# A two-layer attention trunk on one core: the high and low halves of the stationary weights stored column by column in turn

## The chip, the core and the metric

The kernel runs on one core of a Trainium2 chip. The metric is the device time of one execution in microseconds, lower is better. Before the change it is 277.55 us, the median of three runs (277.17 to 279.52). A profiled execution of the same program gives one trace, and the rows further down are read from it.

## The reference

The input is 256 tokens of 1024 features. Two mixer layers follow each other, each ending in a residual layer normalization. In short:

```python
def mla_mixer(x, ...):                  # layer A
    h = x @ w_in                        # 1024 -> 768 + 256 + 32 + 1024
    c_q, c_kv, k_rope, gate = split(h)
    q = rms_norm(c_q) @ w_uq            # 16 heads of 64 + 32
    kv = rms_norm(c_kv) @ w_ukv         # 16 heads of 64 (key) + 64 (value)
    o = causal_softmax_attention(q, k, v)
    return (o * silu(gate)) @ w_o
def moba_mixer(x, ...):                 # layer B, keys and values from x after layer A
    q, gate = split(x @ w_in)           # 1024 -> 1024 + 1024
    o = causal_softmax_attention(rope(q), rope(x @ w_k), x @ w_v)
    return (o * silu(gate)) @ w_o
x = layer_norm(2 ** 0.5 * x + mixer(x)) # ALPHA = 4 ** 0.25
```

With 256 tokens and blocks of 256 the block selection of layer B selects nothing beyond a token's own block, so the kernel computes a causal attention there.

## The kernel before

**Three passes for a product.** TensorE multiplies in a reduced float32 (`fp32r`). To keep accuracy each operand is split into a high half h, rounded to that type, and a low half l, the rest; a product is the sum of three matmuls, h·h, h·l and l·h. The helper `split` (line 445 and the lines around it) makes the halves: ScalarE copies the source into h with the rounding (line 397), then VectorE or GpSimd subtracts h from the source into l (line 408). `passes` (around line 434) issues the three matmuls, all of them recorded under line 427.

**Two kinds of products.** In a `chunk` the weights are the stationary operand: 128 columns of the weights are loaded into the array, and 256 token columns of the activations stream past. Its three loads are h, h and l of the weights. The matmul groups `g1`, `ga`, `qr`, `kq`, `qb`, `kb` and `gb` are of this kind; a matmul of theirs has 256 streamed columns. In `token_products` (`uv`, `oa`, `vb`, `ob`) the activations are stationary, and the weights stream past, 512 columns in most matmuls. For `oa` and `ob` the stationary operand is the gated attention output, kept as `big_h` and `big_l`; for `uv` and `vb` it is `act_h` and `act_l`, which the change leaves alone.

**Weights.** `weights` walks through a list of units (`ORDER`) of 128 partitions by 1024 columns (768 for `qr`, 512 for `kr`). A DMA on SP's queue loads a unit into one of five `raw` buffers, `split` writes h into one of six buffers named `wh` and l into one of six named `wl`. Within a buffer the columns lie side by side, 4 bytes apart, and begin at an offset that depends on the kind of unit (`AT_W`, 8 to 24 elements). The unit `kr` is an exception: its h and l lie in runs of 64 columns in one `wh` buffer. The last two units of `oa`, `vb` and `ob` go into `x_h` and `x_l`.

**Order.** All operations are recorded first, with a table of which view each writes and reads. `Schedule.order` then lists them by a cost model, and each engine's queue runs in the listed order. GpSimd has eight of the sixteen subtractions into `big_l` (the entries `og` of the table `POOL`) and none of the weights'.

Of the kernel before, what the change touches and what calls it, by code (L numbers as in the profile page):

```python
# [8 lines left out]
F32R = mybir.dt.float32r  # L9
# [4 lines left out]
P = 128  # L14
D = 1024
S = 256
# [6 lines left out]
SCALE_B = 64.0 ** -0.5  # L23
# [5 lines left out]
HL_BUFS = 6  # L29
G_BUFS = 5  # L30
LAG = 8
# [20 lines left out]
HEAT = 12  # L52
PAIR = 1.1

AT_ACT, AT_W = 8, {"g1": 24, "ga": 24, "qr": 10, "kq": 10, "qb": 10, "kb": 10, "gb": 10, "uv": 8, "oa": 8, "vb": 8, "ob": 8}
SHIFT = ("x_h", "x_l", "act_h", "act_l", "big_h", "big_l", "wh", "wl")
PLAIN = 2
PIECES = 4
LATE = 2000
# [4 lines left out]
def on(*key):  # L64
    return "pool" if key in POOL else "dve"
# [3 lines left out]
class Val:  # L69
# [9 lines left out]
    def tile(self):  # L79
        if self.t is None:  # L80
            if self.bank:
                self.t = self.pool.tile(self.shape, self.dtype, tag=self.tag, name=self.tag, bufs=self.bufs)
            else:

                n, line = int(np.prod(self.shape[1:])), 64 if self.dtype is BF16 else 32
                room = -(-n // line) * line + line * (self.tag in SHIFT)
                t = self.pool.tile([P, room], self.dtype, tag=self.tag, name=self.tag, bufs=self.bufs)[:, self.at0:self.at0 + n]
                if len(self.shape) > 2:
                    names = "abc"[:len(self.shape) - 1]
                    t = t.rearrange("p (%s) -> p %s" % (" ".join(names), " ".join(names)), **dict(zip(names[1:], self.shape[2:])))  # L90
                self.t = t
        return self.t
# [272 lines left out]
def trunk(ctx, tc, W0, xtok, W, gq, gkv, lng, lnb, cosa, sina, coska, sinka, cosb, sinb, maskd, identd, out):  # L365
# [3 lines left out]
    wp = ctx.enter_context(tc.tile_pool(name="wp", bufs=1))  # L369
# [85 lines left out]
    U = {name: u for u, name in enumerate(ORDER)}  # L455
    hls = {}
    extra = {}
    state = {"raw": 0, "hl": 0}
    raws = {}

    def load_raw():
# [13 lines left out]
    def weights(name, k):  # L475
        u = U[name, k]
        while state["hl"] <= u:
            v = state["hl"]
            if v not in raws:
                load_raw()  # L480
            nm, kk = ORDER[v]
            n = {"qr": 768, "kr": 512}.get(nm, 1024)
            if nm == "kr":
                hl = sc.val(wp, [P, 1024], F32R, "wh", HL_BUFS).rearrange("p (a b c) -> p a b c", b=2, c=64)
                r = raws.pop(v)[:, 0:n].rearrange("p (a c) -> p a c", c=64)
                split(hl[:, :, 0, :].at(0), hl[:, :, 1, :].at(1), r, n)
                hls[v] = hl.rearrange("p a b c -> p a (b c)")
                state["hl"] += 1
                continue
            if nm in ("oa", "vb", "ob") and kk >= 6:  # L490
                if kk == 6:
                    extra["h"] = C([P, 2, 1024], "x_h", F32R, AT_W[nm])
                    extra["l"] = C([P, 2, 1024], "x_l", F32R, AT_W[nm])
                h, l = extra["h"][:, kk - 6].at(kk), extra["l"][:, kk - 6].at(kk)
            else:
                h = sc.val(wp, [P, 1024], F32R, "wh", HL_BUFS, AT_W[nm])[:, :]
                l = sc.val(wp, [P, 1024], F32R, "wl", HL_BUFS, AT_W[nm])[:, :]
            r = raws.pop(v)
            parts = [(c, c + S) for c in range(S * (v < PLAIN), n, S)] if v < PIECES else [(0, n)]
            for c0, c1 in parts:  # L500
                cs, rs = slice(c0, c1), slice(c0 + S * (v < 8), c1 + S * (v < 8))
                split(h[:, cs].at((kk, c0)), l[:, cs].at((kk, c0)), r[:, rs].at(512 if v < PLAIN else 0), c1 - c0, eng=on("w", nm, kk))
            hls[v] = (h, l, kk, v < PIECES)
            state["hl"] += 1
        return hls[u]

    def wsl(w, c0, c1):
        h, l, kk, early = w
        key = (kk, c0 // S * S if early else 0)
        return h[:, c0:c1].at(key), l[:, c0:c1].at(key)  # L510


    def const(src, shape, name, rows=None):
# [55 lines left out]
    g1 = [bank("s"), bank("s"), bank("pt"), bank("pt")]  # L569
# [8 lines left out]
    for k in range(8):  # L578
        w = weights("g1", k)
        a, b = xs(k)  # L580
        for c in range(8):
# [5 lines left out]
            h, l = wsl(w, c * P, (c + 1) * P)  # L587
# [37 lines left out]
    for j in range(6):  # L625
        b, c = 1 + j // 2, j % 2
# [139 lines left out]
            r.append(t)  # L766
        return r

    def values(la, ps_, pts, Vt, ogh, ogl):

        ps, calls, used = bank("pv"), [], []
        for j, p in enumerate(ps_):
            for t in range(2):
                for s in range(2):
                    v = Vt[:, t, 2 * p + s, :].at((t, (2 * p + s) // 8))
                    calls.append((ps[64 * s:64 * s + 64, j * S + t * P:j * S + S], v, pts[j][s][:, t * S:S + t * P], t == 0, t == 1))
                    used += [v, pts[j][s]]
        mms(calls, ps, used, 250 + 642 * len(ps_))
        for j, p in enumerate(ps_):
            oa = T([P, S], "oa")  # L780
            tt(oa, ps[:, j * S:(j + 1) * S], Gs.pop(p), ALU.mult, S)
            split(ogh[:, p, :].at(p), ogl[:, p, :].at(p), oa, S, eng=on("og", la, p))

    def value_evac(Vt, banks, tok):
        for hf in range(2):
            src = banks[hf].rearrange("p (a b) -> p a b", b=64)
            act(Vt[:, tok, 8 * hf:8 * hf + 8, :].at((tok, hf)), src, 512)

    def attention(la, heads, fill, scale, Vt, ogh, ogl):
        done = []  # L790
        for i in range(8):
            hd, keys = heads(i)
            es = scores(la, i, hd, keys, scale)
            fill(i)
            if len(done) == 2:
                values(la, (i - 2, i - 1), done, Vt, ogh, ogl)
                done = []
            done.append(transp(es))
        values(la, (6, 7), done, Vt, ogh, ogl)

    def heads_mla(p):
        b = p % 4
# [3 lines left out]
    sca = row_power(qsq, 768, "sca")  # L806
    ts(sca, sca, -SCALE_A, None, ALU.mult, None, 2, "pool")
    masks = const(maskd, [P, S], "masks")
    ogh, ogl = C([P, 8, S], "big_h", F32R, AT_ACT), C([P, 8, S], "big_l", F32R, AT_ACT)
    kq_mla(0)  # L810
    kq_mla(1)
    V = C([P, 2, H, 64], "V")
# [10 lines left out]
            else:  # L823
                gate("ga", i, xs)

    attention("a", heads_mla, fill_a, [sca[:, 1:2], sca[:, 0:1]], V, ogh, ogl)


    def load_ln(layer):
# [16 lines left out]
        for hf, cs in enumerate(cols):  # L846
            stt(z[:, cs].at(hf), z[:, cs].at(hf), mv[:, 3:4].at(2), bb[:, cs], ALU.mult, ALU.add, 512)

    def lhs_of(th, tl):
        return lambda k, tok: tuple(t[:, k, tok * P:(tok + 1) * P].at(k) for t in (th, tl))  # L850

    x1h, x1l = C([P, 8, S], "act_h", F32R, AT_ACT), C([P, 8, S], "act_l", F32R, AT_ACT)
    gb, bb = load_ln(0)
# [18 lines left out]
    def x1s(k):  # L872
        return x1h[:, k, :], x1l[:, k, :]

    token_products("oa", 8, lhs_of(ogh, ogl), (("proj", "proj"), ("s", "s")), LAG, finish_a)
    VB = C([P, 2, H, 64], "V")
    token_products("vb", 8, lhs_x1, (("proj", "proj"), ("pv", "proj")), LAG, lambda tok, bk: value_evac(VB, bk, tok))
    gb, bb = load_ln(1)
# [45 lines left out]
    ogh2, ogl2 = C([P, 8, S], "big_h", F32R, AT_ACT), C([P, 8, S], "big_l", F32R, AT_ACT)  # L924

    def fill_b(step):
        for nm, i in PLAN_B[step + 1]:
# [5 lines left out]
        move_heads(step)  # L933

    fill_b(-1)
    attention("b", heads_moba, fill_b, [-SCALE_B, -SCALE_B], VB, ogh2, ogl2)

    def finish_b(tok, bk):
        layer_norm(bk, x1[tok], x1[tok], gb, bb)
# [38 lines left out]
    token_products("ob", 8, lhs_of(ogh2, ogl2), (("proj", "proj"), ("s", "s", "proj")), LAG, finish_b, last_b)  # L978
    sc.emit()


# [89 lines left out]
```

## Time and profile before

| what | value |
|---|---|
| median of 3 runs | 277.55 us (277.17 to 279.52) |
| the profiled execution | 277.43 us |
| its span in the trace | 275.3 us |
| around the span | 2.1 us |
| TensorE, matmuls (PE) | 265.9 us busy, 97% of the span, 1948 matmuls |
| TensorE, weight loads (PEld) | 244.8 us busy, 89%, 1948 loads |
| VectorE (DVE) | 209.2 us, 76% |
| ScalarE (ACT) | 159.8 us, 58% |
| GpSimd (POOL) | 56.7 us, 21% |

A matmul's record is longer than the time by which it holds up the next one, because matmuls overlap in the array. So the pace of TensorE is read from the number of matmuls in a stretch of time, not from the length of one. Each matmul has a weight load of its own, whose record lies beside the matmul ahead of it.

### The profile page before, as it was taken

How to read it: one execution, taken by the hardware profiler on the slowest of the kernel's cores; microseconds unless marked ns; L12 is line 12 of the kernel's file. 1: busy time of each engine (PE TensorE's matmuls, PEld its weight loads, DVE VectorE, ACT ScalarE, POOL GpSimd, SP SyncE). 2: the span in 40 equal slices, each digit the busy share in tenths (PEclk: the TensorE clock that was granted, in tenths of full speed). 3: DMA queues.
4: the chain of work that ended last, by engine and by line, in shares of the span. 5: the costliest groups of instructions: out<-in, count | busy, mean ns of one | idle time of the engine just before them, and what ended most of it. 6: DMA issues, size and time to landing. Idle time of an engine off the chain costs nothing.

```text
span 275.3 us, 5378 instructions
## 1 busy us (share of the span) xinstructions
PE 265.9 (97%) x1948; PEld 244.8 (89%) x1948; DVE 209.2 (76%) x458; ACT 159.8 (58%) x338; POOL 56.7 (21%) x72
## 2 busy tenths in 40 slices
PE   8999999999999999999999999999999999999990
PEld 6999999899899998788878899999999999887880
DVE  2778798999986668828995727869888978684655
ACT  4767877686766678706244734547746858592000
POOL 3000163300130253001010000604133446321100
PEclk9999999999999999999999999999999999999996
DMA  7999855786426342232689776467769577430012
GB/s 235 388 393 341 300 166 177 226 270 192 155 77 195 120 148 76 97 134 79 207 267 339 219 267 185 161 170 226 240 160 353 143 276 243 118 103 2 0 76 76
DMA packets 18681, 52.31 MB, mean 190 GB/s; under 512 B 2912, under 2 KB 6112, under 8 KB 18656
## 3 DMA queue, kind: packets, MB, share of 16 engines
q1 hardware_dynamic: 18656, 51.98, 56.8%
q8 instruction: 15, 0.25, 0.4%
q14 instruction: 10, 0.08, 0.1%
HBM read 45.68 MB, written 1.05 MB: 170 GB/s over the span
## 4 chain that ended last, share of the span: by engine, by line
PE 89%; DVE 5%; DMA 1%; ACT 1%; issue 1%; SPq 0%; POOL 0%; DVEq 0%
PE proj L427 58%; PE s L427 15%; PE pv L427 8%; PE pt L427 4%; PE pt L441 4%; DVE wl L408 2%; DMA kq<-x_h 1%; DVE m L412 1%; DVE act_h L412 1%; SPq L389 0%; DVE bst L840 0%; ACT wh L397 0%; POOL mv L408 0%; ACT pt L397 0%; DVE act_l L408 0%
## 5 line engine op out<-in xcount | busy, mean ns | idle before, releaser
L408 DVE TENSOR_TENSOR wl<-raw,wh 128x1024 fp32r<-128x1024 f32 (+2 forms) x82 | 87.6, 1086 | 22.3 <-ACT wh L397 22.0
L397 ACT CAST wh<-raw 128x1024 fp32r<-128x1024 f32 (+3 forms) x83 | 75.5, 923 | 36.9 <-PE proj L427 15.7
L427 PE MATMUL proj<-act_h,wh 128*128 128x256 f32 x280 | 79.9, 285 | 0.0
L427 PE MATMUL proj<-act_h,wl 128*128 128x256 f32 x280 | 78.4, 280 | 0.0
L427 PE MATMUL proj<-act_l,wh 128*128 128x256 f32 x280 | 78.2, 279 | 0.0
L427 PEld LDWEIGHTS proj<-act_l,wh 128*128 128x128 f32 x280 | 52.9, 189 | 0.0
L427 PEld LDWEIGHTS proj<-act_h,wl 128*128 128x128 f32 x280 | 52.6, 188 | 0.0
L427 PEld LDWEIGHTS proj<-act_h,wh 128*128 128x128 f32 x280 | 52.6, 188 | 0.0
L401 ACT ACTIVATE e<-e,st 128x256 f32<-128x256 f32 x64 | 28.6, 450 | 8.8 <-DVE st L746 8.4
L421 POOL TENSOR_SCALAR e<-e,st 128x256 f32<-128x256 f32 (+1 forms) x32 | 16.0, 515 | 49.1 <-PE s L427 24.6
L427 PE MATMUL s<-kq 128*128 128x256 f32 (+1 forms) x100 | 18.9, 316 | 0.5 <-DMA kq<-x_h 0.5
L427 PE MATMUL proj<-x_h,wh 128*128 128x256 f32 x64 | 18.7, 292 | 0.0
L427 PE MATMUL proj<-x_l,wh 128*128 128x256 f32 x64 | 18.0, 281 | 0.0
L427 PE MATMUL proj<-x_h,wl 128*128 128x256 f32 x64 | 17.9, 280 | 0.0
L427 PEld LDWEIGHTS s<-kq 128*128 128x128 f32 x100 | 15.7, 190 | 2.0 <-PE pt L441 0.7
L397 ACT COPY pt<-pt 128x384 f32<-128x384 f32 x32 | 14.8, 474 | 3.5 <-PE pt L441 3.5
L441 PE MATMUL pt<-ident,e 128*128 128x128 f32 x96 | 15.1, 275 | 0.0
L408 POOL TENSOR_TENSOR t<-t,t512b 128x512 f32<-128x512 f32 x5 | 6.8, 1365 | 31.6 <-DVE t L408 13.9
L746 DVE CUSTOM_DVE_ANT_0 e<-s,masks,sca 128x256 f32<-128x256 f32 (+1 forms) x32 | 11.9, 412 | 1.7 <-POOL e L421 0.5
L408 DVE TENSOR_TENSOR x_l<-raw,x_h 128x256 fp32r<-128x256 f32 (+1 forms) x14 | 10.4, 764 | 3.5 <-ACT x_h L397 3.4
L408 POOL TENSOR_TENSOR mv<-mv,mhalf 128x1 f32<-128x1 f32 x4 | 3.5, 870 | 44.3 <-DVE mv L419 36.1
L408 POOL TENSOR_TENSOR x_h<-t,x_h 128x512 fp32r<-128x512 f32 x7 | 11.0, 1589 | 7.3 <-ACT x_h L397 4.0
(166 smaller groups left out, 567.1 us busy)
## 6 DMA issues: line engine op xcount, KB each, us to landing
raw<-in_W SPq DMA_DIRECT2D x66, 512.0 KB, 4.6
raw<-in_W SPq DMA_DIRECT2D x6, 640.0 KB, 7.4
raw<-in_W SPq DMA_DIRECT2D x6, 384.0 KB, 4.0
kq<-x_h SPq DMA_DIRECT2D x24, 96.0 KB, 2.2
kq<-x_h SPq DMA_DIRECT2D x24, 64.0 KB, 2.1
lng<-in_lng SPq DMA_DIRECT2D x2, 512.0 KB, 3.6
lnb<-in_lnb SPq DMA_DIRECT2D x2, 512.0 KB, 5.0
raw<-in_xtok SPq DMA_DIRECT2D x2, 512.0 KB, 3.7
```

Of the source, the lines that this page charges most:

```text
L397: nc.scalar.copy(A(o), A(i))
L401: nc.scalar.activation(A(o), A(i), func, bias=A(bias), scale=A(scale), accum_out=A(accum))
L408: sc.op(eng, dur, lambda: e.tensor_tensor(A(o), A(a), A(b), op=op), [a, b], [o], lock=not (is_ps(a) or is_ps(b)))
L412: sc.op("dve", dur, lambda: nc.vector.scalar_tensor_tensor(A(o), A(a), A(s), A(b), op0=op0, op1=op1), [a, s, b], [o], lock=not (is_ps(a) o ...
L421: fn = lambda: e.tensor_scalar(A(o), A(a), A(s1), s2, op0=op0, op1=op1)
L427: nc.tensor.matmul(A(out_), A(lt), A(rh), start=st, stop=sp_, skip_group_check=True)
L441: nc.tensor.transpose(A(x), A(y), A(ident))
L746: nc.vector.tensor_tensor_reduce(A(e[:, cs]), A(ps[:, cs]), A(msk), scale=A(scale[b]), scalar=3.0e38, op0=ALU.add, op1=ALU.min, accum_out= ...
```

## The change

The two rings `wh` and `wl` become one ring `w` of six buffers with 2048 columns each. In units whose weights are stationary, h and l of a column are neighbours: h of column c lies at element 2c, l at 2c + 1, so that the columns of either half are 8 bytes apart. The unit's start within its buffer is no longer set by its kind but by the number of the buffer: 0, 12, 22, 32, 44 or 54 elements, that is 0, 48, 88, 128, 176 or 216 bytes. Units whose weights stream past (`uv`, `oa`, `vb`, `ob`) keep two contiguous halves in their buffer. The gated attention output becomes one tensor `big` with h and l in turn in the same way; it is the stationary operand of `oa` and `ob`.

Every engine has the same instructions in the same order as before, with other names and addresses. One thing about the waits differs: in eight of VectorE's subtractions into l, and in one of ScalarE's instructions, a wait for TensorE is no longer listed, since h and l now lie in one buffer and an earlier instruction already waits for it.

```diff
-AT_ACT, AT_W = 8, {"g1": 24, "ga": 24, "qr": 10, "kq": 10, "qb": 10, "kb": 10, "gb": 10, "uv": 8, "oa": 8, "vb": 8, "ob": 8}
-SHIFT = ("x_h", "x_l", "act_h", "act_l", "big_h", "big_l", "wh", "wl")
+AT_ACT, AT_W = 8, 8
+PHASE = (0, 12, 22, 32, 44, 54)
+SHIFT = ("x_h", "x_l", "act_h", "act_l", "big")
...
-                room = -(-n // line) * line + line * (self.tag in SHIFT)
+                room = -(-n // line) * line + line * (self.tag in SHIFT) + 64 * (self.tag == "w")
...
-                hl = sc.val(wp, [P, 1024], F32R, "wh", HL_BUFS).rearrange("p (a b c) -> p a b c", b=2, c=64)
+                hl = sc.val(wp, [P, 2048], F32R, "w", HL_BUFS)[:, 0:1024].rearrange("p (a b c) -> p a b c", b=2, c=64)
+                state["used"] += 1
...
-                h = sc.val(wp, [P, 1024], F32R, "wh", HL_BUFS, AT_W[nm])[:, :]
-                l = sc.val(wp, [P, 1024], F32R, "wl", HL_BUFS, AT_W[nm])[:, :]
+                token = nm in ("uv", "oa", "vb", "ob")
+                t = sc.val(wp, [P, 2048], F32R, "w", HL_BUFS, AT_W if token else PHASE[state["used"] % HL_BUFS])
+                state["used"] += 1
+                t = t.rearrange("p (b c) -> p b c" if token else "p (c b) -> p b c", b=2)
+                h, l = t[:, 0], t[:, 1]
...
-            split(ogh[:, p, :].at(p), ogl[:, p, :].at(p), oa, S, eng=on("og", la, p))
+            split(og[:, p, :, 0].at((p, 0)), og[:, p, :, 1].at((p, 1)), oa, S, eng=on("og", la, p))
...
-    ogh, ogl = C([P, 8, S], "big_h", F32R, AT_ACT), C([P, 8, S], "big_l", F32R, AT_ACT)
+    og = C([P, 8, S, 2], "big", F32R, AT_ACT)
...
-    def lhs_of(th, tl):
-        return lambda k, tok: tuple(t[:, k, tok * P:(tok + 1) * P].at(k) for t in (th, tl))
+    def lhs_of(t):
+        return lambda k, tok: tuple(t[:, k, tok * P:(tok + 1) * P, i].at((k, i)) for i in range(2))
```

## Rows read from the trace of the kernel before

**Rows 1.** The page: busy time of each engine; granted clock by slices; the chain.

```profile
PE 265.9 (97%) x1948; PEld 244.8 (89%) x1948; DVE 209.2 (76%) x458; ACT 159.8 (58%) x338; POOL 56.7 (21%) x72
...
PEclk9999999999999999999999999999999999999996
...
PE 89%; DVE 5%; DMA 1%; ACT 1%; issue 1%; SPq 0%; POOL 0%; DVEq 0%
```

**Rows 2.** Pieces of the chain in order of time: start, length in us, what.

```profile
71.26 1.31 PE s L427 x8
...
123.64 5.59 PE s L427 x24
...
144.96 4.86 PE proj L427 x21
...
159.55 26.52 PE proj L427 x225
...
265.00 2.83 PE proj L427 x24
```

**Rows 3.** Timeline at 44 us, TensorE: start, length in us, engine, instructions merged.

```profile
44.05 0.53 PEld L427 LDWEIGHTS proj<-ones,lnb 128*128 128x128 f32 x4
44.16 0.50 PE L427 MATMUL proj<-ones,lnb 128*128 128x1 f32 x4
```

**Rows 4.** Groups by form, weight loads: count, busy us, mean ns of one.

```profile
L427 PEld LDWEIGHTS proj<-act_h,wh 128*128 128x128 f32 x280 | 52.6, 188 | 0.0
...
L427 PEld LDWEIGHTS pv<-pt,V 128*64 128x64 f32 x128 | 7.9, 136 | 3.8 <-issue 0.7
```

**Rows 5.** Groups by form, matmuls with stationary weights; each stands for three.

```profile
L427 PE MATMUL proj<-act_h,wh 128*128 128x256 f32 x280 | 79.9, 285 | 0.0
...
L427 PE MATMUL proj<-x_h,wh 128*128 128x256 f32 x64 | 18.7, 292 | 0.0
...
L427 PE MATMUL pt<-x_h,wh 128*128 128x256 f32 x32 | 8.8, 280 | 0.0
...
L427 PE MATMUL s<-x_h,wh 128*128 128x256 f32 x28 | 8.0, 290 | 0.0
```

**Rows 6.** Groups by form on VectorE, ScalarE and GpSimd: splits and their like.

```profile
L408 DVE TENSOR_TENSOR wl<-raw,wh 128x1024 fp32r<-128x1024 f32 x64 | 78.8, 1240 | 20.1 <-ACT wh L397 19.9
...
L408 DVE TENSOR_TENSOR wl<-raw,wh 128x256 fp32r<-128x256 f32 x14 | 5.0, 419 | 2.1 <-ACT wh L397 2.1
...
L397 ACT CAST wh<-raw 128x1024 fp32r<-128x1024 f32 x64 | 67.0, 1047 | 34.5 <-PE proj L427 15.7 <-PE s L427 9.1 <-DMA raw<-in_W 6.6
...
L408 POOL TENSOR_TENSOR t<-t,t512b 128x512 f32<-128x512 f32 x5 | 6.8, 1365 | 31.6 <-DVE t L408 13.9 <-DVE st L752 9.2 <-DVE t512b L408 8.4
...
L408 POOL TENSOR_TENSOR big_l<-oa,big_h 128x256 fp32r<-128x256 f32 x8 | 6.5, 824 | 18.8 <-ACT big_h L397 18.8
```

**Rows 7.** Busy time by stages; columns PE, PEld, DVE, ACT, POOL, clock, DMA.

```profile
0.00:28.00 28.00, 26.96 (x207) 25.58 (x208) 18.51 (x38) 18.65 (x37) 2.08 (x6) 1.00 0.92 338
28.00:56.00 28.00, 28.00 (x216) 26.97 (x216) 24.82 (x39) 20.45 (x34) 9.28 (x7) 1.00 0.64 211
56.00:110.00 54.00, 54.00 (x442) 51.28 (x442) 44.58 (x129) 39.60 (x107) 10.89 (x22) 1.00 0.49 156
...
158.00:243.00 85.00, 84.53 (x720) 82.25 (x719) 66.11 (x161) 52.26 (x118) 30.16 (x32) 1.00 0.66 210
```

**Rows 8.** The same stages, VectorE's subtractions into `wl` alone.

```profile
28.00:56.00 28.00, 10.49 (x10) 1.00 0.64 211
56.00:110.00 54.00, 16.77 (x14) 1.00 0.49 156
...
158.00:243.00 85.00, 30.30 (x24) 1.00 0.66 210
```

**Rows 9.** Who waited for whom: us in total, times, longest.

```profile
DVE wl L408 <- ACT wh L397: 22.0, 26, 4.2
...
ACT wh L397 <- PE proj L427: 15.7, 12, 2.1
```

More of the change, by code (lines that the diff above doesn't have):

```diff
@@ L457, in trunk @@
     extra = {}
-    state = {"raw": 0, "hl": 0}
+    state = {"raw": 0, "hl": 0, "used": 0}
     raws = {}
@@ L491, in weights @@
                 if kk == 6:
-                    extra["h"] = C([P, 2, 1024], "x_h", F32R, AT_W[nm])
-                    extra["l"] = C([P, 2, 1024], "x_l", F32R, AT_W[nm])
+                    extra["h"] = C([P, 2, 1024], "x_h", F32R, AT_W)
+                    extra["l"] = C([P, 2, 1024], "x_l", F32R, AT_W)
                 h, l = extra["h"][:, kk - 6].at(kk), extra["l"][:, kk - 6].at(kk)
             else:
-                h = sc.val(wp, [P, 1024], F32R, "wh", HL_BUFS, AT_W[nm])[:, :]
-                l = sc.val(wp, [P, 1024], F32R, "wl", HL_BUFS, AT_W[nm])[:, :]
+                token = nm in ("uv", "oa", "vb", "ob")
[3 more added lines that the diff above has]
+                h, l = t[:, 0], t[:, 1]
             r = raws.pop(v)
@@ L501, in weights @@
                 cs, rs = slice(c0, c1), slice(c0 + S * (v < 8), c1 + S * (v < 8))
-                split(h[:, cs].at((kk, c0)), l[:, cs].at((kk, c0)), r[:, rs].at(512 if v < PLAIN else 0), c1 - c0, eng=on("w", nm, kk))
+                split(h[:, cs].at((kk, c0, 0)), l[:, cs].at((kk, c0, 1)), r[:, rs].at(512 if v < PLAIN else 0), c1 - c0, eng=on("w", nm, kk))
             hls[v] = (h, l, kk, v < PIECES)
@@ L509, in wsl @@
         key = (kk, c0 // S * S if early else 0)
-        return h[:, c0:c1].at(key), l[:, c0:c1].at(key)
+        return h[:, c0:c1].at(key + (0,)), l[:, c0:c1].at(key + (1,))
     def const(src, shape, name, rows=None):
@@ L767, in transp, with values @@
         return r
-    def values(la, ps_, pts, Vt, ogh, ogl):
+    def values(la, ps_, pts, Vt, og):
         ps, calls, used = bank("pv"), [], []
@@ L787, in value_evac, with attention @@
             act(Vt[:, tok, 8 * hf:8 * hf + 8, :].at((tok, hf)), src, 512)
-    def attention(la, heads, fill, scale, Vt, ogh, ogl):
+    def attention(la, heads, fill, scale, Vt, og):
         done = []
@@ L795, in attention @@
             if len(done) == 2:
-                values(la, (i - 2, i - 1), done, Vt, ogh, ogl)
+                values(la, (i - 2, i - 1), done, Vt, og)
                 done = []
             done.append(transp(es))
-        values(la, (6, 7), done, Vt, ogh, ogl)
+        values(la, (6, 7), done, Vt, og)
     def heads_mla(p):
@@ L824, in fill_a @@
                 gate("ga", i, xs)
-    attention("a", heads_mla, fill_a, [sca[:, 1:2], sca[:, 0:1]], V, ogh, ogl)
+    attention("a", heads_mla, fill_a, [sca[:, 1:2], sca[:, 0:1]], V, og)
     def load_ln(layer):
@@ L873, in x1s @@
         return x1h[:, k, :], x1l[:, k, :]
-    token_products("oa", 8, lhs_of(ogh, ogl), (("proj", "proj"), ("s", "s")), LAG, finish_a)
+    token_products("oa", 8, lhs_of(og), (("proj", "proj"), ("s", "s")), LAG, finish_a)
     VB = C([P, 2, H, 64], "V")
@@ L922, in heads_moba @@
                 for s in range(2)], keys
-    ogh2, ogl2 = C([P, 8, S], "big_h", F32R, AT_ACT), C([P, 8, S], "big_l", F32R, AT_ACT)
+    og2 = C([P, 8, S, 2], "big", F32R, AT_ACT)
     def fill_b(step):
@@ L935, in trunk @@
     fill_b(-1)
-    attention("b", heads_moba, fill_b, [-SCALE_B, -SCALE_B], VB, ogh2, ogl2)
+    attention("b", heads_moba, fill_b, [-SCALE_B, -SCALE_B], VB, og2)
     def finish_b(tok, bk):
@@ L976, in last_b @@
             dma(out[1][:, q * S:q * S + S], y[:, q * S:q * S + S], 1024 * P, r=[y.at(q)])
-    token_products("ob", 8, lhs_of(ogh2, ogl2), (("proj", "proj"), ("s", "s", "proj")), LAG, finish_b, last_b)
+    token_products("ob", 8, lhs_of(og2), (("proj", "proj"), ("s", "s", "proj")), LAG, finish_b, last_b)
     sc.emit()
```

## The prediction

> **What bounds the kernel now.** I read the page first. PE is busy for 97% of the span at the full 2.4 GHz level of the clock, and PE makes up 89% of the chain that ended last [rows 1]; so what counts is the time by which one matmul holds up the next. That is read from the pieces of the chain [rows 2]. The piece of 225 matmuls with 256 streamed columns takes 26.52 us, 117.9 ns each. The 24 matmuls at 265 us, when ScalarE and the transfers are almost done, take 2.83 us, also 117.9 ns. So the pace does not depend on what the other engines read and write. Pieces with 512 streamed columns give 4.86 / 21 = 231.4 ns and 5.59 / 24 = 232.9 ns.
>
> Next, what the 117.9 ns are made of. At 2.4 GHz 256 columns take 106.7 ns. The 256 columns that a 512-column matmul has more cost 231.4 - 117.9 = 113.5 ns, and during these no weight load is due, since each matmul has one load only. So 113.5 ns is the price of 256 streamed columns by themselves, and 117.9 - 113.5 = 4.4 ns is left for whatever comes once a matmul. Part of it is fixed: the eight matmuls at 71.26 us take float32 in two half-rate passes, four of them with 256 columns and four with 128, 1,536 columns or 1,280 ns at half rate, and their piece has 1.31 us; 30 ns over eight matmuls leaves up to 3.8 ns for each [rows 2]. The weight load is the other suspect. With one streamed column, four loads take 0.53 us with the last one's 0.19 us in it, so they follow each other at (0.53 - 0.19) / 3 = 113 ns [rows 3]. A load of 64 columns is recorded 52 ns shorter than one of 128 [rows 4], so a load reads a column in about 0.81 ns. A 256-column matmul therefore has its stream at 113.5 ns and its load at 113 ns side by side, both near 118, and any clash between the two reads shows at once.
>
> **The change, part by part.** *Reading the weights, step 8 bytes.* The products with stationary weights are 280 + 64 + 32 + 28 groups of three [rows 5], 1,212 loads; with `oa` (96) and `ob` (120), whose stationary `big` is stepped too, 1,428. Their streamed operands stay contiguous, and so do the stationary operands of `uv` and `vb`. Today the load goes 4 bytes further per 0.81 ns and the stream 4 bytes per 0.44 ns, so the load falls behind and the distance between their addresses runs through 512 bytes during each load. With the step the load goes 8 bytes per 0.81 ns, the pace of the stream, and the distance stays nearly what it was at the start. If part of the 4.4 ns is clashes at certain distances, most loads lose it: a stream that has been held up once is out of the other's way and stays so. No row has a stepped load. The bounds are a gain of 4.4 ns (the stream alone sets the pace; 113 ns for the load alone forbids more) and, on the other side, a loss as large, if the distance stays at a bad value. I take half the gain, 2.2 ns, because part of the 4.4 is fixed. The first 28 us get nothing: transfers fill 92% of them [rows 7], and 3 x (32 + 28) = 180 matmuls of `g1` run there at the pace of the arriving weights. So 1,428 - 180 = 1,248 matmuls x 2.2 ns = 2.7 us, nearly all on the chain.
>
> [...]
>
> *Writing the halves.* ScalarE writes h in steps of 8 bytes, 1,047 ns for 1,024 columns today, and VectorE reads that h and writes l in steps, 1,240 ns [rows 6]. The slope on VectorE is (1,240 - 419) / 768 = 1.07 ns a column. A gain is out, as the engines process one column at a time whatever the step. The nearest row of an engine that works slower per column is GpSimd's, (1,365 - 824) / 256 = 2.11 ns, so the extra cost lies between 0 and 1.04 ns a column. I take 0, since all columns still go through one after the other on the same 128 partitions, and keep the other end as a rival. What covers a small loss is the idle quarter of VectorE and the idle 42% of ScalarE [rows 1]; where it is used up, I say below. The eight subtractions on GpSimd into `big` (824 ns each) are few, and the matmuls on `big` come after whole steps of attention.
>
> *One ring for both halves.* h may now be overwritten only when the last load of l is done, one matmul later than before: 12 waits of ScalarE for PE [rows 9] x 0.118 us = 1.4 us of ScalarE's idle time. Behind the waiting copy stand ScalarE's other copies, and VectorE's subtraction into l, which waits for h anyway. The buffer is needed five units later, some 5 x 24 x 0.118 = 14 us, which hides it; without that cover it would cost at most 1.4 us. That VectorE no longer lists its own wait for PE frees nothing, as the same subtraction waits for ScalarE (26 waits, [rows 9]). The other addresses (`raw` 128 bytes lower, offsets by buffer) add no instruction.
>
> *Sum.* The profiled execution has 277.43 us, 0.12 under the median. 277.43 - 2.75 = 274.7; from the median 274.8 us.
>
> **The rivals.** *Nothing happens.* The 4.4 ns are the fixed part of a matmul, of which the half-rate piece allows up to 3.8; then the layout has nothing to win or lose, and the time stays at 277.5, give or take 1.5. For it speaks that the pace is the same to 0.1 ns in the two pieces of [rows 2], whatever offsets their buffers have.
>
> *Load and stream stay in each other's way (slower).* The same equal pace works against the kernel if a load begins at an address that clashes with the stream's and neither is moved off. Six offsets spread over 216 bytes make it likely that some buffers begin badly. It decides from the point at which bad buffers cost more than good ones gain; at its far bound all 1,248 matmuls lose 4.4 ns, 5.5 us, which gives 283; with 2.2 ns it is 280.3. Against it: today each load runs through every distance, good and bad, and pays no more than 4.4 ns for all of them.
>
> *Stepped writes slow the splits (slower).* Then VectorE becomes the bound in the stages where its slack is small [rows 7, 8]. From 28 to 56 us it has 28 - 24.82 = 3.2 us left for 10 subtractions: this decides from 3.2 / (10 x 1,024) = 0.31 ns a column. From 56 to 110 us it is 9.4 us for 14 (0.66 ns), from 158 to 243 us 18.9 us for 24 (0.77 ns). At the far bound of 1.04 ns the stages run over by 7.5, 5.5 and 6.7 us: 297 us. At half of that only the first stage runs over, by 2.1 us; with imperfect overlap I allow some 6 us, 283. [...]
>
> *The load halves its rate.* A load that takes one column in twice the time lasts some 104 ns longer, and every one of the 1,248 matmuls waits for it: about 130 us more, 407 us. Only the missing row speaks for it.
>
> *More is won than the clash.* If the stream's 113.5 ns themselves hang on the load, the floor is the load's 113 ns today, so again near 272; less only if a stepped load were faster than a contiguous one.
>
> **How the numbers follow.** The forecast (clashes go, 272.0 to 277.0) has a chance of 0.43, nothing (within 1.5 us of 277.5) 0.25, clashes that stay 0.15, slower splits 0.11, a load at half rate 0.03, more won than 5.5 us 0.03. The predicted time is 274.8 us. The range is 270.8 to 284.0: it takes in the whole bound of the gain, the far bound of the clashes and half of that of the splits, and leaves out the half-rate load, the worse half of slow splits and the largest gains. A measurement of this kernel tells a change of about 1% from none, 2.8 us; that puts 274.8 just at the edge. Below it lies a good half of the forecast, and what is won beyond: faster 0.39. The rest of the forecast, nothing, and the small clashes: same 0.37. Slower 0.24.
>
> **What would show it.** Right: the piece of 225 matmuls falls from 26.52 to about 26.0 us (115.7 ns), `vb`'s 231.4 ns stays, the load's record stays near 188 ns, the subtraction stays near 1,240 ns and the copy near 1,047 ns. If clashes depend on the distance alone, matmuls of different buffers will now differ in pace, where today they don't. Wrong: a subtraction well over 1,300 ns, or idle time of PE that VectorE ends; a pace of 120 ns and more; a pace below 113 ns, which would mean that the stream's price of 113.5 ns was the load's doing after all.

## The result, and the profile after

The changed kernel takes 280.02 us (median of 16 runs, 279.23 to 281.41) against 277.96 us (16 runs, 276.91 to 280.03) for the kernel before: ratio 1.0068, 95% interval 1.0048 to 1.0089. It is slower, by some 2 us (0.7%); the forecast was 2.75 us faster. The ratios further down are each taken against executions of the kernel before from the same round, without those in the chip's slower state (medians 277.8 to 278.4 us).

The page of the profile after, against [rows 1]: busy time, clock by slices, chain.

```profile
PE 268.4 (97%) x1948; PEld 248.7 (90%) x1948; DVE 208.6 (75%) x458; ACT 164.6 (59%) x338; POOL 57.3 (21%) x72
...
PEclk9999999999999999999999999999999999999998
...
PE 92%; DVE 5%; issue 1%; ACT 1%; POOL 0%; DVEq 0%
```

The clock is the same, and PE has an even larger share of the chain. No other engine took over; PE's own work became longer. The same pieces of the chain as in [rows 2]:

```profile
30.20 26.64 PE proj L429 x200
...
125.04 5.56 PE s L429 x24
...
146.37 4.88 PE proj L429 x21
161.03 26.87 PE proj L429 x225
...
266.92 2.89 PE proj L429 x24
```

The piece of 225 matmuls now has 119.4 ns for each instead of 117.9, the 24 at the end 120.4 instead of 117.9. The two pieces with 512 streamed columns, the first with stepped loads and the second with contiguous ones, show no loss (231.7 and 232.4 ns; 232.9 and 231.4 before). So the loss lies where 256 columns stream past a stepped load. Taken over the whole trace, from the starts of the matmul records: the mean gap behind a matmul of 256 fp32r columns, over the 1,290 gaps between 100 and 140 ns, is 118.0 ns before and 119.8 after. 1.8 ns x 1,290 = 2.3 us, and at 227 us after the first matmul the changed kernel is indeed 2.33 us behind; after that it gets some 0.5 us back, because the 3.64 us that the chain of before spent on a transfer at 231.68 us are not in the chain after.

The groups of the weight loads, against [rows 4]: stationary weights in steps, then a stationary operand that stayed contiguous.

```profile
L429 PEld LDWEIGHTS proj<-act_h,w 128*128 128x128 f32 x560 | 90.5, 196 | 0.0
...
L429 PEld LDWEIGHTS proj<-w,act_h 128*128 128x128 f32 x52 | 9.7, 188 | 2.7 <-DVE w L410 0.5
```

A stepped load is recorded 8 ns longer (196 against 188); the contiguous one is as before. Of the splits, against [rows 6], ScalarE's became longer (1,115 against 1,047 ns, with the units that stayed contiguous in the mean), VectorE's did not (1,232 against 1,240):

```profile
L399 ACT CAST w<-raw 128x1024 fp32r<-128x1024 f32 x64 | 71.3, 1115 | 34.9 <-PE proj L429 15.5 <-PE s L429 9.0 <-DMA raw<-in_W 7.2
...
L410 DVE TENSOR_TENSOR w<-raw,w 128x1024 fp32r<-128x1024 f32 x64 | 78.4, 1232 | 22.1 <-ACT w L399 21.9
```

### The profile page after: what moved, and what is told of

Its sections match the earlier page's. It is cut to its first block, busy times and chain, and to the rows that moved or that the text cites. A ratio compares the mean times of both kernels' runs of the same rounds, so it can differ in the third digit from the quotient of the medians.

```text
span 277.3 us, 5376 instructions
## 1 busy us (share of the span) xinstructions
PE 268.4 (97%) x1948; PEld 248.7 (90%) x1948; DVE 208.6 (75%) x458; ACT 164.6 (59%) x338; POOL 57.3 (21%) x72
## 4 chain that ended last, share of the span: by engine, by line
PE 92%; DVE 5%; issue 1%; ACT 1%; POOL 0%; DVEq 0%
PE proj L429 60%; PE s L429 16%; PE pv L429 8%; PE pt L429 4%; PE pt L443 4%; DVE w L410 2%; DVE m L414 1%; DVE act_h L414 1%; DVE bst L847 0%; ACT w L399 0%; POOL mv L410 0%; DVE act_l L410 0%; ACT act_h L399 0%; DVE bst L958 0%; DVEq L1074 0%
## 5 line engine op out<-in xcount | busy, mean ns | idle before, releaser
L429 PE MATMUL proj<-act_h,w 128*128 128x256 f32 x560 | 106.1, 284 | 0.0
L410 DVE TENSOR_TENSOR w<-raw,w 128x1024 fp32r<-128x1024 f32 (+3 forms) x83 | 87.8, 1076 | 23.9 <-ACT w L399 23.3
L399 ACT CAST w<-raw 128x1024 fp32r<-128x1024 f32 (+3 forms) x83 | 80.2, 982 | 36.5 <-PE proj L429 15.5
L429 PEld LDWEIGHTS proj<-act_h,w 128*128 128x128 f32 x560 | 90.5, 196 | 0.0
L429 PE MATMUL proj<-act_l,w 128*128 128x256 f32 x280 | 79.3, 283 | 0.0
L429 PEld LDWEIGHTS proj<-act_l,w 128*128 128x128 f32 x280 | 54.9, 196 | 0.0
L429 PE MATMUL proj<-x_h,w 128*128 128x256 f32 x128 | 25.9, 289 | 0.0
L429 PEld LDWEIGHTS proj<-x_h,w 128*128 128x128 f32 x128 | 21.3, 198 | 0.2 <-issue 0.2
L429 PE MATMUL proj<-w,big 128*128 128x512 f32 (+1 forms) x90 | 21.0, 379 | 0.0
L429 PE MATMUL proj<-x_l,w 128*128 128x256 f32 x64 | 18.1, 283 | 0.0
```

The costliest lines, as they stand in the source:

```text
L399: nc.scalar.copy(A(o), A(i))
L410: sc.op(eng, dur, lambda: e.tensor_tensor(A(o), A(a), A(b), op=op), [a, b], [o], lock=not (is_ps(a) or is_ps(b)))
L429: nc.tensor.matmul(A(out_), A(lt), A(rh), start=st, stop=sp_, skip_group_check=True)
```

## The experiments

The theories: **A**, an engine that passes 16 bytes more often than once in some 1.77 ns (113.5 ns for the stream's 256 columns of 4 bytes, by 64) is held up, whatever lies beside it. **B**, the loads clash with the stream at certain address distances. **C**, each stepped instruction pays a fixed price. **D**, ScalarE's longer copies delay the chain. **E**, the ring with its common release costs the time, not the layout.

**steps: the disputed prices by themselves.** Blocks of 24 matmuls on the same two arrays, and of four elementwise instructions, one source line each, for example

```
for i in range(24): nc.tensor.matmul(ps[0:128, 0:256], A[:, 0 + (i % 2) * 256:0 + (i % 2) * 256 + 255:2], B[:, 0:256], ...)
for i in range(4): nc.scalar.copy(Y[:, 0:2047:2], X[:, 0:1024])
```

> This kernel leaves the computation out: it runs blocks of 24 matmuls and of 4 elementwise instructions, one source line for each block, and measures the disputed prices by themselves. Theory A (a reader or writer that comes to a new 16-byte line more often than about once in 1.77 ns is held up, so step 8 bytes is just too fast for an engine with 0.83 ns a column): loads alone take 113 ns apart at step 4 bytes, 121 at 8, some 170 at 12 and 227 at 16; loads of 64 columns 57 and 61; ScalarE's copy of 1,024 columns takes 1.05, 1.14, 1.36 and 1.81 us, VectorE's subtraction 1.22 at step 8 and 1.8 at step 16; matmuls of 256 columns follow at 118 ns with contiguous loads and at 121 or more with stepped ones at every offset; a streamed operand of one repeated column takes 213 instead of 231 ns for 512 columns. Theory B (distance: a load in step with the stream stays in its way where it begins badly): loads alone keep 113 ns at step 8; the pace of 256-column matmuls with stepped loads runs from 118 to 122 ns with the offset, and stays flat with contiguous loads. Theory C (each stepped instruction pays a fixed price at its start): loads 121 ns at steps 8, 12 and 16 alike, 65 for 64 columns, copies the same at all steps above 4 bytes.

Groups by form of this kernel; L78 to L81 are ScalarE's copies of 1,024 columns, written in steps of 4, 8, 12 and 16 bytes, L84 and L87 to L89 VectorE's subtractions with one operand read and the result written in the same four steps:

```profile
L81 ACT CAST Y<-X 128x1024 fp32r<-128x1024 f32 x4 | 8.2, 2059 | 0.1
...
L80 ACT CAST Y<-X 128x1024 fp32r<-128x1024 f32 x4 | 6.4, 1594 | 0.1
L79 ACT CAST Y<-X 128x1024 fp32r<-128x1024 f32 x4 | 4.5, 1133 | 0.1
...
L78 ACT CAST Y<-X 128x1024 fp32r<-128x1024 f32 x4 | 4.2, 1045 | 0.1
```

```profile
L89 DVE TENSOR_TENSOR Z<-X,X 128x1024 fp32r<-128x1024 f32 x4 | 8.1, 2017 | 0.1
L88 DVE TENSOR_TENSOR Z<-X,X 128x1024 fp32r<-128x1024 f32 x4 | 6.2, 1562 | 0.1
L87 DVE TENSOR_TENSOR Z<-X,X 128x1024 fp32r<-128x1024 f32 x4 | 4.9, 1226 | 0.1
...
L84 DVE TENSOR_TENSOR Z<-X,X 128x1024 fp32r<-128x1024 f32 x4 | 4.9, 1224 | 0.1
```

From step 12 to 16 ScalarE needs (2,059 - 1,594) / 1,024 = 0.45 ns more a column, VectorE 0.44: 4 bytes more at one price, which makes 1.82 and 1.78 ns for 16 bytes. At step 8 that would be 0.9 ns a column. VectorE takes 1.07 ns a column anyway [rows 6] and notices nothing (1,226 against 1,224 ns); ScalarE's 1,133 - 1,045 = 88 ns are 0.09 ns a column. This fits theory A, on two engines (I had put 16 bytes at 1.77 ns and so the last copy at 1.81 us, without the start that every copy has, some 190 ns by the 1,047 and 403 ns for 1,024 and 256 columns in the kernel before); C, the same price at all steps, falls. What is shown is a price that grows with the bytes passed. The lines of 16 bytes in the expectations are an assumption of mine: no step here is over 16 bytes, and no run tests them.

Pieces of the chain of the same kernel: start, length, line. L34 streams 512 contiguous columns past contiguous loads. L35, L36 and L38 are loads with four streamed columns in steps of 4, 8 and 16 bytes. L47 streams 256 columns in steps of 8 bytes, L48 and L50 one repeated column 512 and 256 times, all three past contiguous loads. L70 is a contiguous load 64 bytes past the stream's place within 512 bytes.

```profile
23.49 5.44 PE ps L34 x24
28.93 2.57 PE ps L35 x24
31.50 3.06 PE ps L36 x24
...
39.69 5.58 PE ps L38 x24
...
79.01 5.44 PE ps L47 x24
84.46 5.25 PE ps L48 x24
...
94.95 2.69 PE ps L50 x24
...
152.27 2.83 PE ps L70 x24
```

Contiguous loads alone follow at 111.7 ns: by the records the first two matmuls of L35 start 28 ns apart and the others 111 to 112, so 2.57 us / 24 = 107.1 is too low. 256 more columns that repeat one column cost (5.25 - 2.69) / 24 = 106.7 ns, while 256 that are read one after another cost 5.44 / 48 = 113.3 in L34 and 113.5 by the prediction's own subtraction: 113.3 ns / 64 stretches of 16 bytes = 1.77 ns, the same price again. In steps of 8 bytes 256 streamed columns take 5.44 / 24 = 226.7 ns, twice that. The granted clock fell during L36, the second block with few streamed columns: its first 21 gaps have 117 to 119 ns, its last two 214 and 215. The stretch of the next block (step 12) has a granted clock of 0.50, and so has that of L38, so TensorE's stepped loads had to be measured again (steps_hot, below).

Three expectations of theory A were missed. The repeated column took 5.25 / 24 = 218.8 ns for 512, not 213. The pace with stepped loads was not 121 ns or more at every offset but ran from 118.0 to 121.7, so B was not out either; and with contiguous loads it was not 118 throughout but 117.1 to 120.0, which B did not expect. The loads of 64 columns (L39 and L40) fell into the stretch with a granted clock of 0.50 and say nothing about steps. The stretches of L37 to L40, the clock in the third column from the right:

```profile
34.70:39.60 4.90, 4.90 (x25) 4.90 (x24) 0.00 (x0) 0.00 (x0) 0.00 (x0) 0.50 0.00 0
39.80:45.20 5.40, 5.40 (x25) 5.40 (x26) 0.00 (x0) 0.00 (x0) 0.00 (x0) 0.50 0.00 0
45.40:47.80 2.40, 2.40 (x25) 2.40 (x24) 0.00 (x0) 0.00 (x0) 0.00 (x0) 0.50 0.00 0
47.90:50.30 2.40, 2.40 (x25) 2.40 (x24) 0.00 (x0) 0.00 (x0) 0.00 (x0) 0.50 0.00 0
```

**contiguous_weights, contiguous_big, stepped_big_only: which part of the change.** The first two are the changed kernel with one edit each (of the second the main line alone is shown; the lines that write and read `big` follow it), the third the kernel before with `big` alone interleaved:

```diff
-                t = t.rearrange("p (b c) -> p b c" if token else "p (c b) -> p b c", b=2)
+                t = t.rearrange("p (b c) -> p b c", b=2)
```

```diff
-    og = C([P, 8, S, 2], "big", F32R, AT_ACT)
+    og = C([P, 8, S], "big_h", F32R, AT_ACT), C([P, 8, S], "big_l", F32R, AT_ACT)
```

> The weights' halves lie contiguous in the one ring again, with its six offsets and its common release; only the array of the gated attention outputs stays interleaved. If the stepped weights are to blame, by their loads (theories A to C) or by ScalarE's copies (theory D), this gives back nearly all: 278.0 to 278.4 us against 277.9 before, ratio 1.000 to 1.002, load records at 188 ns, the piece of 225 matmuls at 26.5 us. If the ring with its common release or the other addresses cost the time (theory E), it stays at 280, ratio 1.007.

> The array of the gated attention outputs lies in two contiguous halves again, the weights stay interleaved. Theories A to C: 216 of the 1,428 stepped loads are gone, and of the 1.5 to 2.1 us only the last piece's 0.06 us and a little of oa come back: 279.6 to 280.0 us, ratio 1.006 to 1.007. If GpSimd's and ScalarE's writes into that array delayed the end of attention, more than half comes back: under 279, ratio under 1.004.

> The kernel before with only the array of the gated attention outputs interleaved. Theories A to C: 216 stepped loads, of which those with 512 streamed columns are covered: 277.9 to 278.3 us, ratio 1.000 to 1.0015; the last 24 matmuls at 120.4 instead of 117.9 ns. If that array is the main cause: 279.5 or more, ratio over 1.005.

Contiguous weights in the changed kernel: 278.03 us, ratio 1.0004 (0.998 to 1.0029). All is given back, within the interval, although ring, offsets and common release stay; E falls. Contiguous `big`: 279.80, ratio 1.0059 (1.0037 to 1.0081). Only `big` in steps: 278.73, ratio 1.0013 (0.9985 to 1.004), which can't be told from nothing, though the median lies above the 277.9 to 278.3 us expected; its last 24 matmuls, on `big`, took 2.90 us, 120.8 ns each, as expected. The weights carry the loss.

**read_stepped, write_stepped: the loads or ScalarE.** The halves are written in one layout and read in the other:

```diff
-                t = t.rearrange("p (b c) -> p b c" if token else "p (c b) -> p b c", b=2)
+                both = token or v < PIECES or nm == "qr"
+                rd = t.rearrange("p (b c) -> p b c" if token else "p (c b) -> p b c" if both else "p (c b) -> p b c", b=2)
+                t = t.rearrange("p (b c) -> p b c" if token else "p (c b) -> p b c" if both else "p (b c) -> p b c", b=2)
...
```

(read_stepped; in write_stepped the two layouts behind `if both else` are swapped. In both, the lines left out make a load of h wait for l as well, because either half may now lie where the other is read. `big` and the units of `qr` stay as in the changed kernel.)

> ScalarE and VectorE write the weights' halves contiguous, the loads read them in steps of 8 bytes; so the products use other columns than the reference's, and the time alone counts. (The first four units, those of qr, and the array of the attention outputs stay as in the changed kernel.) Theories A and B (the loads are to blame): 279.5 to 280.2 us, ratio 1.005 to 1.008, copies at 1,050 ns, load records at 196. Theory D (ScalarE's longer copies delay the chain): 278.0 to 278.4, ratio under 1.003.

> ScalarE and VectorE write the weights' halves in steps of 8 bytes, the loads read contiguous stretches; so the products use other columns than the reference's, and the time alone counts. (The same parts stay as in the changed kernel.) Theories A and B: the loads record 188 ns, the piece of 225 is back at 26.5 us, 278.0 to 278.5 us, ratio 1.000 to 1.003, although the copies take 1,140 ns. Theory D: 279.5 to 280.2, ratio 1.005 to 1.008.

Groups of read_stepped, loads and copies:

```profile
L429 PEld LDWEIGHTS proj<-act_h,w 128*128 128x128 f32 x560 | 90.5, 196 | 0.0
```

```profile
L399 ACT CAST w<-raw 128x1024 fp32r<-128x1024 f32 x64 | 67.1, 1048 | 40.2 <-PE proj L429 14.8 <-PE s L429 12.6 <-DMA raw<-in_W 9.2
```

The same of write_stepped:

```profile
L429 PEld LDWEIGHTS proj<-act_h,w 128*128 128x128 f32 x560 | 88.3, 189 | 0.0
```

```profile
L399 ACT CAST w<-raw 128x1024 fp32r<-128x1024 f32 x64 | 71.3, 1114 | 37.7 <-PE proj L429 13.4 <-DMA raw<-in_W 11.7 <-PE s L429 9.0
```

With stepped loads and quick copies: 280.38 us, ratio 1.0077 (1.0048 to 1.0106), the whole loss. With contiguous loads and slow copies: 278.53, ratio 1.0004 (0.9979 to 1.0028), none. D falls: 67 ns a copy are covered by ScalarE's idle time, as the prediction said of a small loss. The loads are to blame.

**good_offsets, bad_offset: the distance.** One offset for all six buffers:

```diff
-                t = sc.val(wp, [P, 2048], F32R, "w", HL_BUFS, AT_W if token else PHASE[state["used"] % HL_BUFS])
+                t = sc.val(wp, [P, 2048], F32R, "w", HL_BUFS, AT_W if token else 4 if nm in ("g1", "ga") else 12)
```

(good_offsets; in bad_offset it is `AT_W if token else 22`.)

> The changed kernel with the same offset in all six buffers: 16 bytes for g1 and ga, 48 bytes for the other products, which puts every stepped load 16 bytes past a 64-byte boundary counted from its streamed operand. Theory B (address distance; the isolated blocks were quickest there, 118.0 to 118.8 ns): the piece of 225 matmuls at 118.0 to 118.5 ns, 26.55 to 26.65 us, time 278.0 to 278.7, ratio 1.000 to 1.003. If every stepped load costs the same wherever it lies: 119.5 ns, 280.0 us, ratio 1.007 as with the six offsets.

> The changed kernel with an offset of 88 bytes in all six buffers, where the loads of the changed kernel had a pace of 120.3 to 122.5 ns. Theory B: the piece of 225 at some 121 ns, 27.2 us, and 1,248 loads x 3 ns give 281 to 282 us, ratio 1.011 to 1.016. If the offset is without effect: 280.0, ratio 1.007.

Good offsets: 279.73 us, ratio 1.0056 (1.003 to 1.0083); bad: 280.84, ratio 1.0104 (1.0068 to 1.014). The piece of 225 in the chain of good_offsets, and in that of bad_offset:

```profile
160.23 26.75 PE proj L429 x225
```

```profile
161.35 27.00 PE proj L429 x225
```

The distance acts, 118.9 and 120.0 ns in this piece, 118.7 and 120.4 over the trace, and 1.1 us between the two medians. But B's numbers were missed on both sides: with the good offsets (1.000 to 1.003 expected) the pace is still above that of before, and the bad offset reached 27.00 us and 280.84 us, not 27.2 and 281 to 282. The profiled execution of good_offsets also has more waits: by 213 us after the first matmul it was 1.04 us behind the kernel before, in the last 50 us it lost 1.5 more, where its chain has transfers into `raw` and `kq`.

**steps_hot: the load alone, in longer blocks.** Blocks of 48, with 512-column matmuls between the first ones:

```
for i in range(48): nc.tensor.matmul(ps[0:128, 0:192], A[:, 0 + (i % 2) * 256:0 + (i % 2) * 256 + 255:2], B[:, 0:1].to_broadcast([P, 192]), ...)
```

> This kernel leaves the computation out too: blocks of 48 matmuls at the full clock, one source line for each. Where the streamed operand is one repeated column of 192 columns' length (80 ns of stream that reads next to nothing), the pace is the price of the load alone. Theory A (a port gets no new 16-byte line within some 1.82 ns, as ScalarE's 2.06 us for 1,024 columns at step 16 bytes say): 107 to 113 ns for the contiguous load, 117 to 118 at step 8, 175 at 12, 233 at 16, and the offset changes nothing there. With a contiguous streamed operand of 256 columns the clash comes on top: 118 ns at the best offset of a stepped load and 121 to 122 at the worst, in a pattern that repeats after 64 bytes and in the second pass; contiguous loads stay within 117 to 120. With 512 columns the load is hidden: 227 ns with either step. Theory B alone: 107 to 113 ns at step 8 with the repeated column, and below 118 at the best offset with the contiguous one.

Pieces of its chain. L36, L38, L40, L42: 192 times one repeated column, loads in steps of 4, 8, 12, 16 bytes. L44 and L45: 256 times, steps of 4 and 8. L50 and L51: 512 contiguous columns, steps of 4 and 8. L54 and L58: 256 contiguous columns, step 8, offsets 16 and 48 bytes. L68 and L72: 256 contiguous columns, step 4, offsets 0 and 64 bytes.

```profile
26.45 5.33 PE ps L36 x48
...
34.58 5.62 PE ps L38 x48
...
43.02 8.23 PE ps L40 x48
...
54.03 11.13 PE ps L42 x48
...
69.50 5.37 PE ps L44 x48
74.87 5.65 PE ps L45 x48
...
100.24 10.88 PE ps L50 x48
111.12 11.20 PE ps L51 x48
...
133.83 5.70 PE ps L54 x48
...
156.81 5.83 PE ps L58 x48
...
214.57 5.74 PE ps L68 x48
...
237.32 5.44 PE ps L72 x48
```

The first four say what a load costs by itself: 111.0, 117.1, 171.5 and 231.9 ns by length and count. The second matmul of each of these blocks starts 82 to 83 ns after the first; behind it the loads follow at 111.7, 117.7, 173.4 and 233.3 ns (the 121 that theory A gave for step 8 in the first round was too much). From step 12 to 16 it is 0.47 ns a column more, 1.9 ns for 16 bytes: about the price of ScalarE and VectorE, on a third engine.

The clock did not hold in all of these blocks. In L42 the granted clock fell to 0.50:

```profile
58.40:65.10 6.70, 6.70 (x30) 6.70 (x30) 0.00 (x0) 0.00 (x0) 0.00 (x0) 0.50 0.00 0
```

Apart from two at the fall itself, the gaps of L42 are 233.3 ns on average before it and after it, as they are in L38 of the first bench, which ran at 0.50 throughout. At step 12 the clock does count: 213.3 ns at 0.50 (L37 of the first bench) against 173.4 at the full clock. So the price of a load in steps of 16 bytes is not one of TensorE's clock.

At step 8 the load is 6 ns dearer, and 117.7 ns (L38, L45) is the floor of every matmul with 256 columns in these blocks: with the repeated column the offsets 0, 16, 32 and 48 bytes gave 117.7 to 117.9. On top of that comes the distance, 118.5 to 121.5 ns with a contiguous stream at 16 offsets (in two passes alike to 0.3 ns). My expectation was off in two places: the pattern did not repeat after 64 bytes (offset 80 bytes had 120.0, not 118), and 512-column matmuls with stepped loads had 233.3 ns against 226.7, so they don't hide everything. And contiguous loads were not within 117 to 120: at a distance of 64 bytes they follow at 113.3 ns (113.5 in the second pass), which is the bare price of the stream (226.7 ns for 512 columns, L50), with nothing left for a clash.

At step 8 VectorE's subtraction is as fast as at step 4 (1,226 against 1,224 ns), TensorE's load (117.7 against 111.7) and ScalarE's copy (1,133 against 1,045) are not. The three rows fit the reading that it depends on how long the engine itself takes for two columns: 2.14 ns on VectorE (2 x 1.07), 1.68 on ScalarE (2 x (1,047 - 403) / 768) and, as an estimate from L39 of the first bench, 1.67 for the load (106.7 ns for 64 columns at a granted clock of 0.50, halved for 1.00 as if it went with the clock), where 16 bytes cost 1.78 to 1.9 ns.

**one_distance_64, one_distance_0: the distance without any step.** All halves contiguous, all arrays padded so that they begin at the same place within 512 bytes; the weights then lie 64 or 0 bytes past the operand streamed against them, in nearly every product with 256 columns:

```diff
-AT_ACT, AT_W = 8, 8
+AT_ACT, AT_W = 16, 0
...
-                room = -(-n // line) * line + line * (self.tag in SHIFT) + 64 * (self.tag == "w")
+                room = -(-n // line) * line + 128 * (self.tag in SHIFT) + 64 * (self.tag in ("x_l", "act_l", "big_l"))
...
-                t = sc.val(wp, [P, 2048], F32R, "w", HL_BUFS, AT_W if token else PHASE[state["used"] % HL_BUFS])
+                t = sc.val(wp, [P, 2048], F32R, "w", HL_BUFS, AT_W if token else 16 if nm in ("g1", "ga") else 32)
```

(one_distance_64, with `w` and both halves of `big` in `SHIFT`; one_distance_0 has 0 and 16 in place of 16 and 32.)

> All halves contiguous, in one ring; all arrays start at the same place within 512 bytes, and the weights 64 bytes past the operand that is streamed against them, so that each load of 128 columns starts at the one distance that gave 113.4 ns in the isolated blocks of contiguous loads. If the distance alone sets the pace: 113.4 to 115 ns, the piece of 225 at 25.5 to 25.9 us, and 272.5 to 275 us, ratio 0.98 to 0.99. The same distance also gave 117.8 ns in a shorter isolated block, so the history of the stream counts too: then 117.9 ns and 277.5 to 278.2 us, ratio 1.000.

> The same kernel with the weights at distance 0 from the streamed operand, where isolated blocks of contiguous loads had 119.6 to 120 ns. If the distance sets the pace in the kernel too: the piece of 225 at 119.5 to 120 ns, 26.9 to 27.0 us, and 279.5 to 280.5 us, as slow as the changed kernel though nothing is stepped, ratio 1.005 to 1.010. If the products of the kernel, with their three loads in a group, take no notice: 26.5 us, 277.5 to 278.2, ratio 1.000.

At distance 0: 280.55 us, ratio 1.009 (1.0059 to 1.012), as slow as the changed kernel although no load is stepped. The piece of 225 of its chain, at 120.0 ns:

```profile
161.16 26.99 PE proj L429 x225
```

At distance 64: 277.19 us, ratio 0.9988 (0.9959 to 1.0018), no difference from the kernel before that can be told, although the pace fell. Pieces of its chain:

```profile
29.83 25.97 PE proj L429 x200
57.10 5.58 PE proj L429 x48
...
98.44 2.73 PE proj L429 x24
...
194.96 4.32 DMA x_l<-x_h
...
204.23 4.22 DMA raw<-in_W
```

2.73 us for 24 are 113.8 ns, 5.58 for 48 are 116.2; over the trace the mean gap is 115.5 against 118.0. 2.5 ns x 1,285 gaps would be 3.2 us. The page's chain tells where most of it went:

```profile
PE 75%; DVE 13%; DMA 3%; ACT 3%; POOL 2%; issue 2%; SPq 1%; DVEq 0%; POOLq 0%; ACTq 0%
```

PE is down from 89% [rows 1] to 75%, VectorE up from 5% to 13%. Quicker products run into the next thing that is late: subtractions into the weights' low halves (5%), and transfers around 200 us. By the records, the gaps over 140 ns behind the same kind of matmul, waits for the most part, grew from 6.9 to 9.6 us in all, and those behind 512 columns by 0.5. At 185 us after the first matmul the kernel was 1.20 us ahead, at the end 0.69.

The mean gap of all kernels, worked out from the matmul records as above (1,283 to 1,290 gaps each):

| kernel | loads | mean gap, ns | ratio |
|---|---|---|---|
| before | contiguous, several distances | 118.0 | 1 |
| changed | step 8, six offsets | 119.8 | 1.0068 |
| contiguous_weights | contiguous, six offsets | 118.3 | 1.0004 |
| write_stepped | contiguous, six offsets | 118.5 | 1.0004 |
| read_stepped | step 8, six offsets | 119.7 | 1.0077 |
| contiguous_big | step 8, six offsets | 119.6 | 1.0059 |
| stepped_big_only | contiguous, several distances | 118.1 | 1.0013 |
| good_offsets | step 8, good distance | 118.7 | 1.0056 |
| bad_offset | step 8, bad distance | 120.4 | 1.0104 |
| one_distance_64 | contiguous, best distance | 115.5 | 0.9988 |
| one_distance_0 | contiguous, bad distance | 119.6 | 1.0090 |

## Why the prediction was wrong

**What held.** PE's pace is the bound, and the loss is a matter of nanoseconds per matmul on 256 columns. The stream's own price is 113.5 ns, as read: L72 of steps_hot, with one load for each matmul like any other, has 113.3, and 24 matmuls of one_distance_64 had 113.8. So hardly anything of the 4.4 ns was the fixed part for which I halved the gain, and the rival that nothing happens, which took all of it for fixed, falls too. The 106.7 ns that the prediction took for 256 columns at the full clock are what 256 columns cost that repeat one column (L48 less L50 of steps, granted clock 1.00). The float32 matmuls of attention do have half the rate: in the trace of before they are two records for each product, and follow at 215 to 219 ns with 256 columns and at 108 to 113 with 128. That the 4.4 ns are clashes is shown as far as the start address moves them; the kernel as a whole did not come below 115.5. VectorE's subtraction stayed near 1,240 ns, and the ring's common release cost nothing that could be seen (contiguous_weights). The pace now differs between buffers, as foretold if clashes depend on distance: from the records, 118.0 ns at a distance of 144 bytes (within 256; 97 matmuls), 122.5 at 216 (47 matmuls); before, no distance with 50 matmuls or more was outside 117.5 to 118.6.

**The step that failed: "with the step the load goes 8 bytes per 0.81 ns".** It took for granted that the load keeps its time per column. No run shows that, and steps_hot shows 117.7 ns for a load at step 8 against 111.7 at step 4. By my estimate the load takes a column in 0.83 ns at best (the estimate from L39 of the first bench), which at step 8 would be 16 bytes in 1.67 ns, and 16 bytes have a price of 1.8 to 1.9. So the load alone goes from 111.7 to 117.7 ns, all of the room in which the 4.4 ns could have been won. (The 113 ns that I read from [rows 3] for a load alone were some 1.5 ns too much.) The bounds of that step were stated for the clash alone ("113 ns for the load alone forbids more"); the price of the stepped load itself had no row and should have had bounds of its own. The row that was nearest was there: the stream reads 16 bytes in 1.77 ns, where a repeated column has 1.67 (106.7 / 64), and the 6.8 ns that this costs on 256 columns were in the prediction as the difference of 113.5 and 106.7, with no cause looked for. This floor explains why nothing was won. It does not explain the loss by itself, as it lies 0.3 ns under the pace of before.

**The second step that failed: "the distance stays nearly what it was at the start", hence clashes vanish.** This is where the 1.8 ns come from. Stepped loads clash in their own way: 118.5 to 121.5 ns by offset, never below the floor. That a stream once held up stays out of the load's way was my assumption, and no run shows it. And today's contiguous loads don't run "through every distance, good and bad" to the same sum: their pace depends on where they start as well (113.3 to 120.2 ns in steps_hot; 116.3 to 120.6 by distance in contiguous_weights; ratio 1.009 for one_distance_0). Six offsets (119.8) came out between good and bad (118.7 and 120.4).

**A term put at nothing.** The prediction left out the 180 matmuls of `g1`, which were to run "at the pace of the arriving weights". They ran at TensorE's own pace: from 3.8 to 27.4 us PE is never idle in either kernel, and the mean gap of `g1` is 118.1 ns before and 120.2 after. One piece of the chain of before, and the same of after:

```profile
18.90 1.41 PE s L427 x12
```

```profile
19.23 1.44 PE s L429 x12
```

So `g1` paid as well; a busy queue of transfers was taken for a wait that no row showed.

**The rival that came true** is the one that load and stream stay in each other's way: 2.2 ns each was priced at 280.3 us, 1.8 ns and 280.02 us were measured. Its mechanism holds in part: of the 1.8 ns, good_offsets keeps 0.7 and the rest goes with the offsets. That the price came so near is partly luck: it is 2.2 ns on 1,248 matmuls, and what was measured is 1.8 ns on 1,290. The rival of slow splits had ScalarE's copies right in sign, at 0.09 ns a column, but they hang on nothing (write_stepped), and 0.31 ns on VectorE was never near (1,226 against 1,224 ns at step 8). That a gain is out held: no step of the first bench made a copy or a subtraction shorter. "Whatever the step" did not: from step 4 to step 16 1,024 columns went from 1,045 to 2,059 ns on ScalarE and from 1,224 to 2,017 on VectorE. The load at half rate does exist, at step 16 (233.3 ns).

**Left open.** Why loads and stream clash at all, why a distance of 64 bytes is free, and why it is not always: the block L70 of the first bench had the same distance and 117.8 ns (2.83 us for 24), L72 and its repetition in steps_hot 113.3 and 113.5. The blocks before them differ, so how the stream got there may count. In the kernels, too, the start of one load does not set its pace: at distance 0 the contiguous loads of before, which lie among loads at other distances, had 117.6 ns (57 matmuls), those of one_distance_0 119.6 (1,189). No run here separates these.

## What to carry to other kernels

Before an operand is laid out in steps, ask for each engine that walks through it whether it will need 16 bytes more often than the once in about 1.8 ns that all three engines showed here; step 8 was free for the engine with 1.07 ns a column and cost 5 to 8% for the two with some 0.83 (ScalarE by its copies, the load by estimate). Where weight load and stream take nearly the same time, compare the pace of isolated blocks at several relative addresses first: here the start address was worth 113 to 120 ns a matmul in isolated blocks, more than the layout. And price what comes next: 2.5 ns a matmul won on TensorE, 3.2 us in all, came out as 0.1%, within the noise; in the profiled execution VectorE and the transfers were right behind.

## What was not expected of the hardware

- One price of 1.77 to 1.9 ns for 16 bytes fits four readers and writers: ScalarE's writes, VectorE's subtraction, TensorE's weight load and its stream. A repeated column streams at 106.7 ns for 256 (the difference of L48 and L50), a contiguous run at 113.3, one in steps of 8 bytes at 226.7.
- Contiguous loads against a contiguous stream: 113.3 ns at a distance of 64 bytes, 119.6 at 0 and 120.0 to 120.2 at 112; with 512 streamed columns a stepped load still costs 6.6 ns (233.3 against 226.7) in the isolated blocks.
- At a granted clock of 0.50 loads of 64 columns took 106.7 ns each with steps of 4 and of 8 bytes (2.56 us for 24), and loads of 128 in steps of 12 bytes 213.3, twice that; contiguous loads of 128 took 111.7 at 1.00. In steps of 16 bytes they took 233.3 at either clock: there the step sets a floor that the clock doesn't move.
